# A weighted sum over eight experts: four terms of each tail token on TensorE, paired tail loads, two tail stores, and six tokens of one round stored from GpSimd

## The chip, the cores and the metric

The kernel runs on one core of a Trainium2 chip. The metric is the device time of one execution in microseconds (us); the median of five runs is compared. Where one execution was profiled, its own time and its span (first to last instruction on the core's engines) are given beside it, and all durations below are from that execution.

The engines of the core that matter here: VectorE (DVE in the profile), TensorE (PE, with its weight loads as PEld), ScalarE (ACT), GpSimd (POOL) and SyncE (SP). SP, ACT and POOL each issue DMA transfers, on a queue of their own (q1, q10 and q0 in the profile), and one set of 16 DMA engines carries all of them.

## The reference

```python
def setup_inputs():
    batch, seq, n_experts, expert_dim = 16, 1024, 8, 512
    ...
def reference(expert_outputs, combine_weights):
    weights = combine_weights[..., np.newaxis]
    return np.sum(expert_outputs * weights, axis=2).astype(np.float32)
```

Each of 16 x 1024 = 16384 tokens has eight rows of 512 float32 numbers and eight weights; the output is the weighted sum of the eight rows. 268 MB are read and 33.5 MB written, and there is no reuse.

## The kernel before

Every one of the 128 partitions owns 128 tokens (`T_P`). 120 of them (`LOOP`) are done in 12 rounds (`ROUNDS`) of ten tokens (`R`), the other eight (`TAIL`) after that, in the *tail*.

**Buffers.** `ring` holds the ten tokens of one round, eight rows each (16 KB for a token and partition). It is a single buffer: as soon as VectorE has finished the tokens of a chunk, SP loads the next round's chunk into their place. The chunks of a round have 4, 4 and 2 tokens (`CHUNKS`). `acc` holds the results of two rounds, ten tokens (of 2 KB each) in each half. `w_t` holds all weights, `w_c` a copy of the weights of two rounds that ScalarE makes for each round (L167).

**A round** (loop at L219, VectorE alone): for each chunk one `tensor_tensor` (L225) multiplies row 0 of all its tokens by their weights, and then seven `scalar_tensor_tensor` for each token (L215, `fused`) multiply a row by its weight and add it to `acc`. The tokens of a pair are taken in turn, so that an instruction doesn't wait for the one just before it. The last term of a token counts up the semaphore `done`, by which everything else knows how many tokens are finished.

**Loads** are issued by SP in the order of the program (`loads_and_last_stores`): each waits for the `done` count of the tokens whose place it takes. After the 36 chunks of the rounds come eight loads of the tail, one for each token `j` (L142); each waits for the token of the last-but-one place in `ring`, `LOOP - R + j + 1`. Then SP issues the store of the last round (L97) and the stores of the tail (L146), each after its wait on `done`. SP is one instruction stream, so all of this keeps its order, and its transfers are worked off in their order by each DMA engine.

**Stores** of rounds 0 to 9 are one transfer each, issued by ScalarE (L97), which then waits for an earlier one to land before it overwrites the weights' copy. The store of round 10 (`ROUNDS - 2`) is cut up: ScalarE issues four tokens and two tokens over all partitions (L173), and the last four as pairs for 8 partitions (L174); GpSimd issues those pairs for the other 120 partitions (`OURS`, L116). GpSimd also issues two tiny loads into `spare` (`turn`, L121, of 4 and 13 partitions), whose data nobody reads. A transfer over 120 partitions is spread over 15 of the 16 DMA engines.

**The tail.** Eight tokens, each a sum of eight terms. The first `pe_e[j]` of them (6, 6, 6, 6, 5, 5, 5, 4) are made by TensorE: ScalarE writes a diagonal matrix with the weight on its diagonal (`diag`, four buffers, L179), and a matmul with the token's row as moving data (L191) adds weight times row into `ps` in PSUM. [...] ScalarE starts on the diagonals only when all parts of round 10's store have landed (`last_out`, `pairs_out`), since VectorE's tail results go into the same places of `acc`. VectorE adds the remaining terms: `fused` with `ps` as the first addend (waiting for `product`, which counts matmuls), then with `acc`. For tokens 2 to 6 every one of these waits for the one before it. For token 7 VectorE starts from `ring` (L259) and adds `ps` at the very end (L266). Tail stores are of 4, 2, 1 and 1 tokens (`tail_stores`).

What decides the place of the PE terms is this list:

```python
    pe_e = [6, 6, 6, 6, 5, 5, 5, 4]
    tail_stores = [(0, 4), (4, 2), (6, 1), (7, 1)]
    diags = [(j, e) for j in range(TAIL) for e in range(pe_e[j])]
```

## Time and profile before

| | |
|---|---|
| median of 5 runs | 707.05 us (706.75 to 707.31) |
| profiled execution: its time / its span | 707.32 us / 705.1 us |
| VectorE busy | 642.9 us, 91% of the span, 898 instructions |
| TensorE busy, all of it in the tail | 39.9 us, 86 passes (43 matmuls) |
| ScalarE busy | 21.2 us, of it 16.9 us for 43 diagonals |
| GpSimd busy | 2.7 us |
| moved by DMA | 302.54 MB, mean 429 GB/s |
| share of 16 DMA engines' time: SP's queue / ACT's / POOL's | 90.0% / 9.2% / 0.3% |

The span is cut into slices in the profile, and the mean busy share of the 16 DMA engines is 9 tenths or more in all of the 40 slices but the last, where it is 8. VectorE is at 9 tenths or so up to the last two slices, where it is at 5; TensorE works only in the last three. So there are two parts: 672 us of rounds in which the DMA engines are full and VectorE nearly so, and a tail of 33 us in which TensorE, VectorE and the DMA engines all have their share. The change touches what happens from 619.7 us on, where round 10 is finished.

### The profile page before, as it was taken

What the parts mean: (1) busy time and instruction counts of PE and PEld (TensorE: products, weight loads), DVE (VectorE), ACT (ScalarE), POOL (GpSimd) and SP (SyncE); (2) the same over time, 40 slices, a digit from 0 to 9 for tenths busy, and PEclk for the clock granted to TensorE, in tenths of its full rate; (3) what the DMA queues carried; (4) which work ended last, traced back from release to release, by engine and by line L of the source; (5) the groups of instructions that cost most, each with busy time, mean ns of one, the idle gap of its engine ahead of it and who ended that gap; (6) DMA issues with size and microseconds to landing.
All of it is one profiled execution on the core that took longest, in us unless ns stands there. A gap on an engine that the chain in (4) does not pass through costs nothing. (4 is left out here: it accounts for less than half of the span.)

```text
span 705.1 us, 1333 instructions
## 1 busy us (share of the span) xinstructions
PE 39.9 (6%) x86; PEld 17.3 (2%) x86; DVE 642.9 (91%) x898; ACT 21.2 (3%) x56; POOL 2.7 (0%) x9
## 2 busy tenths in 40 slices
PE   0000000000000000000000000000000000000696
PEld 0000000000000000000000000000000000000242
DVE  0599999989999989989989998998998998999955
ACT  0000000000000000000000000000000000000242
POOL 0000000000000000000000000000000000000000
PEclk9999999999999999999999999999999999999998
DMA  9999999999999999999999999999999999999998
GB/s 413 390 472 417 398 437 444 416 448 426 435 434 459 423 412 448 435 425 464 434 393 463 420 424 438 465 402 465 420 445 418 420 431 431 468 407 413 435 429 347
DMA packets 9690, 302.54 MB, mean 429 GB/s; under 512 B 1240, under 2 KB 1624, under 8 KB 2392
## 3 DMA queue, kind: packets, MB, share of 16 engines
q1 hardware_dynamic: 7600, 273.68, 90.0%
q10 hardware_dynamic: 1752, 27.85, 9.2%
q0 software_dynamic: 336, 0.98, 0.3%
q14 instruction: 2, 0.02, 0.0%
HBM read 268.96 MB, written 33.55 MB: 429 GB/s over the span
## 5 line engine op out<-in xcount | busy, mean ns | idle before, releaser
L215 DVE SCALAR_TENSOR_TENSOR acc<-ring,w_c,acc 128x512 f32<-128x512 f32 x840 | 559.7, 747 | 1.3
L225 DVE TENSOR_TENSOR acc<-ring,w_c 128x2048 f32<-128x2048 f32 (+1 forms) x36 | 69.6, 1933 | 43.6 <-DVEq L201 43.6
L191 PE MATMUL ps<-ring,diag 128*128 128x512 f32 x86 | 39.9, 628 | 658.5 <-DMA ring<-in_expert_outputs_dram 658.5
L191 PEld LDWEIGHTS ps<-ring,diag 128*128 128x128 f32 x86 | 17.3, 203 | 680.2 <-DMA ring<-in_expert_outputs_dram 658.5
L167 ACT COPY w_c<-w_t 128x80 f32<-128x80 f32 x12 | 3.0, 258 | 587.1 <-DMA out_dram<-acc 564.8
L179 ACT ACTIVATE diag<-ident,w_t 128x128 f32<-128x128 f32 x43 | 16.9, 400 | 86.2 <-DMA out_dram<-acc 64.4
L215 DVE SCALAR_TENSOR_TENSOR acc<-ring,w_t,ps 128x512 f32<-128x512 f32 x7 | 5.1, 747 | 12.6 <-PE ps L191 12.6
L215 DVE SCALAR_TENSOR_TENSOR acc<-ring,w_t,acc 128x512 f32<-128x512 f32 x13 | 9.7, 751 | 0.4
L116 POOL DMA_DIRECT2D out_dram<-acc x1 | 0.8, 754 | 617.5 <-DVE acc L215 617.5
L167 ACT ACT_TABLE_LOAD x1 | 1.3, 1283 | 0.9 <-SPq L270 0.9
L121 POOL DMA_DIRECT2D spare<-in_combine_weights_dram x2 | 1.3, 645 | 0.3 <-issue 0.3
L266 DVE TENSOR_TENSOR acc<-acc,ps 128x512 f32<-128x512 f32 x1 | 0.7, 689 | 0.1
L259 DVE TENSOR_SCALAR acc<-ring,w_t 128x512 f32<-128x512 f32 x1 | 0.5, 482 | 0.0
L150 POOL TENSOR_SCALAR_AFFINE_SELECT ident<-ident 128x128 f32<-128x128 f32 x1 | 0.3, 287 | 0.1
L149 POOL MEMSET ident<- 128x128 f32 x1 | 0.2, 204 | 0.5 <-SPq L270 0.5
L291 POOL MEMSET const-bfloat16-1.0<- 128x1 bf16 x1 | 0.1, 96 | 0.0
L291 POOL MEMSET const-uint8-127<- 128x1 uint8 x1 | 0.1, 96 | 0.0
L291 POOL MEMSET const-float32-0.0<- 128x1 f32 x1 | 0.1, 93 | 0.2 <-issue 0.2
L291 POOL MEMSET const-float32-1.0<- 128x1 f32 x1 | 0.1, 93 | 0.0
## 6 DMA issues: line engine op xcount, KB each, us to landing
ring<-in_expert_outputs_dram SPq DMA_DIRECT2D x12, 4096.0 KB, 34.0
out_dram<-acc ACTq DMA_DIRECT2D x10, 2560.0 KB, 26.7
ring<-in_expert_outputs_dram SPq DMA_DIRECT2D x8, 2048.0 KB, 29.5
out_dram<-acc SPq DMA_DIRECT2D x1, 2560.0 KB, 26.8
out_dram<-acc ACTq DMA_DIRECT2D x1, 1024.0 KB
out_dram<-acc SPq DMA_DIRECT2D x1, 1024.0 KB, 17.3
out_dram<-acc POOLq DMA_DIRECT2D x1, 960.0 KB, 33.6
out_dram<-acc ACTq DMA_DIRECT2D x1, 512.0 KB
```

What stands on the lines that cost most here:

```text
L116: gpsimd.dma_start(out=o_r[0:OURS], in_=a_r[0:OURS]).then_inc(pairs_out, 16)
L121: gpsimd.dma_start(out=spare[0:k, b : b + 4].rearrange("p (i j) -> p i j", i=2)[:, :, 0:1], in_=w[0 : 2 * k].rearrange("(p i) e -> p i e", ...
L149: gpsimd.memset(ident, 0.0).then_inc(id_set, 1)
L150: gpsimd.affine_select(out=ident, in_=ident, compare_op=mybir.AluOpType.not_equal, fill=1.0, base=0, pattern=[[-1, P]], channel_multiplier ...
L167: scalar.copy(out=w_c[:, h * R : h * R + R], in_=w_t[:, n * R : n * R + R]).then_inc(w_set[h], 1)
L179: i = scalar.mul(out=diag[:, k % DIAGS], in_=ident, mul=w_t[:, LOOP + j, e : e + 1])
L191: tensor.matmul(ps[:, j], lhsT=diag[:, k % DIAGS], rhs=ring[:, j, e], start=e == 0, stop=e == pe_e[j] - 1,).then_inc(product, 1)
L215: return vector.scalar_tensor_tensor(out=acc[:, g], in0=ring[:, g % R, e], scalar=weight, in1=before, op0=mult, op1=add)
L225: i = vector.tensor_tensor(out=acc[:, q : q + m], in0=ring[:, r : r + m, 0], in1=w_c[:, q : q + m, 0:1].to_broadcast([P, m, D]), op=mult,)
L259: i = vector.tensor_scalar_mul(out=acc[:, j], in0=ring[:, j, e], scalar1=weight)
L266: i = vector.tensor_tensor(out=acc[:, j], in0=acc[:, j], in1=ps[:, j], op=add)
L291: nc = _bacc.Bacc("TRN2", target_bir_lowering=False, num_devices=1)
```

## The change

Four things are changed, and all of them lie behind round 10.

1. TensorE makes the first four terms of each tail token (`K = 4`) in place of 6, 6, 6, 6, 5, 5, 5, 4. That is 32 matmuls and 32 diagonals in place of 43, and 33 VectorE instructions in the tail in place of 22.
2. The first six tail tokens are loaded as three pairs. A pair waits for the `done` count of its second token. There are five loads and five semaphores in place of eight.
3. The tail is stored as two transfers of four tokens.
4. Round 10's ten tokens are taken as two halves of five. ScalarE stores the first two of each half, over all partitions, in one transfer. GpSimd stores the last three of each half (six tokens, rows of 6 KB): first for 120 partitions, then, after a tiny load of 5 partitions, for the other 8. ScalarE waits for its own transfer and for GpSimd's four (two tiny loads, two stores) before it starts on the diagonals.

```diff
+    SPLIT = 2
...
-    pe_e = [6, 6, 6, 6, 5, 5, 5, 4]
-    tail_stores = [(0, 4), (4, 2), (6, 1), (7, 1)]
-    diags = [(j, e) for j in range(TAIL) for e in range(pe_e[j])]
+    K = 4
+    tail_loads = [(0, 2), (2, 2), (4, 2), (6, 1), (7, 1)]
+    tail_stores = [(0, 4), (4, 4)]
+    diags = [(j, e) for j in range(TAIL) for e in range(K)]
...
-    tail_in = [sem(f"tail_in{j}") for j in range(TAIL)]
+    tail_in = [sem(f"tail_in{k}") for k in range(len(tail_loads))]
...
+    def halves(n, first, last):
         s = n % 2 * R
-        for r, m in ((0, 4), (6, 2)):
-            yield o_g[n // 4, n // 2 % 2, :, s + r : s + r + m], acc[:, s + r : s + r + m]
-        pairs = [
-            a[:, s + 2 : s + 10].rearrange("p (b k) d -> p b (k d)", k=4)[:, :, 2 * D :]
+        return [
+            a[:, s : s + R].rearrange("p (b k) d -> p b (k d)", b=2)[:, :, first * D : last * D]
             for a in (o_g[n // 4, n // 2 % 2], acc)
         ]
...
+    def store_halves(gpsimd):
+        o_r, a_r = halves(ROUNDS - 2, SPLIT, R // 2)
         turn(gpsimd, 4, 0)
         gpsimd.wait_ge(done, (ROUNDS - 1) * R)
-        o_r, a_r = list(parts(ROUNDS - 2))[2]
-        gpsimd.dma_start(out=o_r[0:OURS], in_=a_r[0:OURS]).then_inc(pairs_out, 16)
-        turn(gpsimd, 13, 4)
+        gpsimd.dma_start(out=o_r[0:OURS], in_=a_r[0:OURS]).then_inc(rest_out, 16)
+        turn(gpsimd, 5, 4)
+        gpsimd.dma_start(out=o_r[OURS:P], in_=a_r[OURS:P]).then_inc(rest_out, 16)
...
-        for j in range(TAIL):
-            sync.wait_ge(done, LOOP - R + j + 1)
-            sync.dma_start(out=ring[:, j], in_=x_t[:, j]).then_inc(tail_in[j], 16)
+        for k, (j, m) in enumerate(tail_loads):
+            sync.wait_ge(done, LOOP - R + j + m)
+            sync.dma_start(out=ring[:, j : j + m], in_=x_t[:, j : j + m]).then_inc(tail_in[k], 16)
...
-        *both, (o_r, a_r) = parts(ROUNDS - 2)
-        for o_p, a_p in both:
-            scalar.dma_start(out=o_p, in_=a_p).then_inc(last_out, 16)
-        scalar.dma_start(out=o_r[OURS:P], in_=a_r[OURS:P]).then_inc(last_out, 16)
-        scalar.wait_ge(last_out, 48)
-        scalar.wait_ge(pairs_out, 48)
+        o_r, a_r = halves(ROUNDS - 2, 0, SPLIT)
+        scalar.dma_start(out=o_r, in_=a_r).then_inc(last_out, 16)
+        scalar.wait_ge(last_out, 16)
+        scalar.wait_ge(rest_out, 64)
...
-            if e == 0:
-                tensor.wait_ge(tail_in[j], 16)
+            if (j, e) in starts:
+                tensor.wait_ge(tail_in[starts[j, e]], 16)
...
-                    if e == pe_e[j]:
+                    if e == K:
                         i = fused(j, e, weight, ps[:, j])
-                        i.wait_op(product, sum(pe_e[: j + 1]), "sem-ge")
+                        i.wait_op(product, K * (j + 1), "sem-ge")
```

The remaining lines of the diff follow from these: `range(K, E)` for `range(pe_e[j], E)`, `stop=e == K - 1`, `starts` (the load that a token's first matmul waits for), `tail_in[-1]` for token 7's first VectorE instruction, and `rest_out` for `pairs_out`.

## The prediction

> **What bounds the kernel now.** I read first the busy time by stretches of the tail, whose columns are the stretch, its length, busy time (and count) of PE, PEld, DVE, ACT and POOL, the granted TensorE clock, the DMA share and GB/s.

> ```profile
> 690.00:692.00 2.00, 2.00 (x6) 0.95 (x5) 1.31 (x2) 1.00 (x3) 0.00 (x0) 1.00 1.08 461
> 698.00:700.00 2.00, 0.34 (x1) 0.00 (x0) 1.93 (x3) 0.00 (x0) 0.00 (x0) 1.00 0.98 412
> ...
> 700.00:701.00 1.00, 0.00 (x0) 0.00 (x0) 0.72 (x2) 0.00 (x0) 0.00 (x0) 1.00 0.99 397
> 701.00:702.00 1.00, 0.00 (x0) 0.00 (x0) 0.00 (x0) 0.00 (x0) 0.00 (x0) 0.74 0.71 272
> 702.00:703.00 1.00, 0.00 (x0) 0.00 (x0) 0.00 (x0) 0.00 (x0) 0.00 (x0) 0.50 0.47 178
> 703.00:704.00 1.00, 0.00 (x0) 0.00 (x0) 0.00 (x0) 0.00 (x0) 0.00 (x0) 0.50 0.02 8
> ```

> The DMA engines are full until 701 and run empty by 703.4. So even a tail without compute could not end much earlier. The chain of waits (start, us, what) tells which compute ends last:

> ```profile
> 630.65 27.76 DMA ring<-in_expert_outputs_dram
> 658.41 0.04 issue
> 658.46 36.46 PE ps L191 x78
> 694.92 0.02 issue
> 694.95 0.76 DVE acc L215
> ...
> 700.14 0.69 DVE acc L266
> ```

> From the landing of token 0 (658.41) to 694.92 TensorE works without a gap; the rest is VectorE. VectorE's timeline shows the same from the other side, as idle time in brackets:

> ```profile
> 673.21 1.41 DVE L215 SCALAR_TENSOR_TENSOR acc<-ring,w_t,acc 128x512 f32<-128x512 f32 x2
> 676.92 0.75 DVE L215 SCALAR_TENSOR_TENSOR acc<-ring,w_t,ps 128x512 f32<-128x512 f32 x1 [2.30 <-PE ps L191]
> ...
> 694.95 0.75 DVE L215 SCALAR_TENSOR_TENSOR acc<-ring,w_t,ps 128x512 f32<-128x512 f32 x1 [1.97 <-PE ps L191]
> 695.73 1.54 DVE L215 SCALAR_TENSOR_TENSOR acc<-ring,w_t,acc 128x512 f32<-128x512 f32 x2
> 697.18 0.48 DVE L259 TENSOR_SCALAR acc<-ring,w_t 128x512 f32<-128x512 f32 x1
> 697.70 2.33 DVE L215 SCALAR_TENSOR_TENSOR acc<-ring,w_t,acc 128x512 f32<-128x512 f32 x3
> 700.14 0.69 DVE L266 TENSOR_TENSOR acc<-acc,ps 128x512 f32<-128x512 f32 x1
> ```

> The last add ends at 700.83, SP issues the last store at 700.85, it lands 3.0 us later (its row in the out_dram view) at 703.84, and 1.29 us of closing work make 705.13. The packets inside those 3.0 us, one per partition: the first start 0.83 us after the issue, an engine has eight of 2 KB at 0.08 us, so most engines are through at 702.4. One DMA engine, still at the earlier tail stores until 702.74, ends at 703.39; 0.45 us later its part has landed. So the compute chain and one late DMA engine end within 1 us of each other.

> **The change, part by part.**

> *Fewer terms on TensorE.* A matmul is two passes, 0.429 us apart at full clock: 11 fewer are 11 x 0.858 = 9.4 us off TensorE. VectorE gets 11 x 0.747 (row of L215) = 8.2 us more. If VectorE never waited from 672.0 (end of its rounds) on: tokens 0 and 1 in turn, 8 x 0.705; tokens 2 to 6, 20 dependent ones at 0.775 (three took 694.95 to 697.27); token 7 as now, 3.56 from the end of token 6 (697.27 to 700.83). Sum 24.7, end at 696.7. That is the floor of this edit, 4.1 us below today's 700.83, if the data were there.

> *Paired loads.* It isn't. A pair is issued with its second token, 0.66 us later than its first now (630.65 and 631.32), which is hidden by the queue in front of it: these loads land 26.5 to 32.5 us after their issue. But the first token of a pair now lands with the second. Issue plus time to landing of tokens 1, 3, 5, 6, 7 today: 631.32 + 32.0 = 663.3, 640.59 + 32.5 = 673.1, 652.20 + 30.7 = 682.9, 660.81 + 27.0 = 687.8, 661.47 + 31.2 = 692.7. Bytes are the same; a 16 KB packet takes 0.611 us and a 32 KB one 1.213, so an engine saves 48 x 0.611 - 24 x 1.213 = 0.2 us.

> *Round 10's store.* For fifteen engines nothing changes in sum: 8 packets of 8 KB (0.309), 8 + 16 of 4 KB (0.159) make 6.3 us; then 16 of 4 KB and 16 of 6 KB (0.234, between the 4 and 8 KB rows) again 6.3. The engine left out has 1.2 us less, but it lands first already (0.7 us ahead of the middle), and a transfer waits for its last engine. The 8 odd partitions put two packets on each of eight engines, 0.47 us now against 0.32; the trace doesn't name the engines, so a late one may gain 0.32 or lose 0.47. With the 0.2 saved, the pair (4, 5) lands between 682.3 and 683.1; I take 682.7, as the late engine is likelier in both groups or in neither than newly in. ScalarE issues two transfers fewer (0.36 to 0.59 us each) and GpSimd one more (0.56 to 0.75); behind them on either engine stand only the waits of the next part, which end 36 us later.

> *The new wait.* ScalarE's diagonals wait for GpSimd's second store too; behind them wait TensorE and VectorE. Today the last part lands at 656.58 and the diagonals start at 656.60. GpSimd's last five queue entries (end marks, tiny load, two rows) now take turns with tail packets of 1.213 instead of 0.611: + 5 x 0.6, plus the larger rows, so about 659.9. Four diagonals (1.28) later it is 661.2, before the pair lands at 663.1: hidden, with 2 us to spare; without that cover it would delay TensorE one for one.

> *The chain.* TensorE starts at 663.2, at half clock for 5.5 us as now (passes 0.853 apart from 658.46 to 663.7). Pair 1's 16 passes: 6.4 slow, 9.6 at 0.429, end 672.8; pair 2 has just landed (672.9) and ends at 679.8; then TensorE stands still for 2.9 us, which it never does now. Token 4's product: 682.7 + 0.05 + 7 x 0.429 + 0.593 (last pass) + 0.04 = 686.4. VectorE is free by then (tokens 0 and 1 until 678.4 since token 1's product comes at 673.4, tokens 2 and 3 until 684.6). Products of tokens 5, 6, 7 follow 3.43 apart: 689.8, 693.3, 696.7, their loads being there. VectorE: token 6 from 693.3, 3.1 us, 696.4; token 7 + 3.56: 699.95. Of the 4.1 us, 0.9 is left: the rest goes into waiting for loads.

> *Two tail stores.* The first four tokens are issued at about 684.6 and wait in the queue anyway. The last store has 1 MB instead of 256 KB: 8 packets of 0.309 = 2.48 against 0.64, so 1.84 us on the path. In return 512 and 256 KB (8 x 0.159 + 8 x 0.08 = 1.9 us) are gone from the queue in front of the late engine, which becomes free at about 700.7 and no longer counts. Sum: 699.95 + 0.02 + 0.83 + 2.48 = 703.28, landing 0.2 to 0.45 later, 1.29 of closing: 704.9. Against the span of 705.13 that is -0.2 us. The profiled execution took 707.32, 0.27 above the median; I take the difference off the median: 706.85.

> *The clock.* The granted clock is the unknown. The stretch 701 to 702 shows 0.74, so full clock ended at 701.5, 3.15 us after the last pass (698.34). A pause of 2.9 us lies just under that, and no shorter one is in the trace. Bounds: nothing (no pause inside the burst now costs any clock), or all of the restart, 5.5 us at half clock = 2.75 us. I take nothing, as the only loss seen came after more.
> [...]

> **The rivals.**

> *The clock drops in the pause* (slower). Place: between pairs 2 and 3. For it: 2.9 against 3.15 us, and the drop's moment needn't be fixed to the burst. Against: the pause is the shorter. Tokens 4 to 7 are chained to it, so all of 2.75 reaches the end: 709.6; with half of it 708.2. It decides from 1.6 us of loss on. 22%.

> *The diagonals come late* (slower). If GpSimd's last rows land after 665, TensorE's first pair ends after 675, and from 1.8 us more (VectorE's slack before token 4, 684.6 against 686.4) the end moves: 3 us late at the end would be 709.9. Against: 3 us of margin in all. 4%.

> *VectorE is the bound and the loads aren't* (faster). Floor 696.7 and the same 4.95 behind it: span 701.65, time 703.6. Against: the DMA share of 0.98 to 1.08 leaves the loads no room to land 4 us earlier. Halfway, with the late engines gone (the middle ones have token 5 at 681.7, 1.2 earlier than the last), it is 705.8, still near my bound. 10% for beyond it.

> *It does as costed*, gains and losses cancelling: 62%, own range 706.0 to 707.7; another 2% I can't name, slower.

> **How the numbers follow.** About 0.2% (1.4 us) is what a measurement of this kernel can tell from no change. Slower than that: 22 + 4 + 2 = 28%; faster 10%; within 62%. The time is the likeliest case's, 706.85. The range goes down to 706.0 (lower bound of the landing, 0.4 earlier, and quicker landing of the last store) and up to 708.7, into the lesser clock losses; some 8% are left out below and 12% above.

> **What would show it.** In the profile after: VectorE through 672 without change; pair landings at 663, 673 and 683; TensorE idle about 2.9 us before pair 3 and full clock behind it; VectorE waiting for TensorE at tokens 4, 5 and 6 and ending near 700; the last store landing 3.5 us or so after its issue; DMA share falling before 700 and rising once more. Wrong: passes 0.85 apart after 683, the first pass well after the first landing, VectorE ending below 698.5, or a last store much longer than 3.6 us.

## The result and the profile after

The changed kernel takes 708.18 us (median of 26 runs) against 706.94 for the kernel before (46 runs): a ratio of 1.0012, 95% interval 1.0006 to 1.0017. That is slower by 0.12%, less than the 0.2% that the prediction took as the bound, but beyond the interval, and the forecast was 706.85, a little faster.

The median hides the main thing. The 26 runs fall into two groups with nothing between them: eight from 706.41 to 706.90 (median 706.5) and eighteen from 708.10 to 708.65 (median 708.2), 1.7 us apart. The kernel before has no such groups (706.63 to 707.34). The profiled execution, 708.37 us with a span of 706.6, is one of the upper group.

The busy time by stretches shows what happened there. The granted clock changes at 682.02 and at 685.44, and 678.61 lies as far ahead of the first change as that from the second; the columns are those of the prediction. Below, a *stretch* is a window of that length, 3.41 us.

```profile
678.61:682.02 3.41, 1.16 (x3) 0.19 (x1) 3.27 (x6) 0.80 (x2) 0.00 (x0) 1.00 0.93 399
682.02:685.44 3.42, 3.09 (x4) 1.50 (x5) 1.50 (x2) 0.40 (x1) 0.00 (x0) 0.50 0.98 414
685.44:690.00 4.56, 4.56 (x12) 1.92 (x11) 2.29 (x4) 2.01 (x5) 0.00 (x0) 1.00 1.03 439
698.00:700.00 2.00, 0.00 (x0) 0.00 (x0) 1.91 (x3) 0.00 (x0) 0.00 (x0) 1.00 0.64 270
700.00:701.00 1.00, 0.00 (x0) 0.00 (x0) 0.89 (x2) 0.00 (x0) 0.00 (x0) 1.00 0.00 0
...
702.00:703.00 1.00, 0.00 (x0) 0.00 (x0) 0.00 (x0) 0.00 (x0) 0.00 (x0) 0.75 1.11 467
703.00:704.00 1.00, 0.00 (x0) 0.00 (x0) 0.00 (x0) 0.00 (x0) 0.00 (x0) 0.50 1.03 418
```

From 682.02 to 685.44 the granted clock is 0.50, with full clock before and after. The pair (4, 5) lands at 682.31, just inside, and its first passes are 0.85 us apart, where they are 0.43 apart behind 685.69. The other new thing is the DMA share: 0.64, then nothing at all from 700 to 701, then full again from 702. The DMA engines, which had work until 701 in the kernel before, now stand still until the packets of the last store start, at 701.99.

The timeline (start, length, engine and line, idle time before in brackets) has the pause and what it does to VectorE:

```profile
662.93 16.84 PE L191 MATMUL ps<-ring,diag 128*128 128x512 f32 x32 [662.93 <-DMA ring<-in_expert_outputs_dram]
...
682.35 15.51 PE L191 MATMUL ps<-ring,diag 128*128 128x512 f32 x32 [2.58 <-DMA ring<-in_expert_outputs_dram]
...
687.60 0.75 DVE L215 SCALAR_TENSOR_TENSOR acc<-ring,w_t,ps 128x512 f32<-128x512 f32 x1 [4.05 <-PE ps L191]
...
700.45 0.69 DVE L266 TENSOR_TENSOR acc<-acc,ps 128x512 f32<-128x512 f32 x1
```

TensorE pauses once, for 2.58 us, before the pair (4, 5). Token 4's product reaches VectorE at 687.60. At full clock it takes 3.74 us from the first pass (682.37 to 686.11 in experiment 4's profile), which would be 686.1; here it took 5.25. The products of tokens 5 and 6 follow 3.44 and 3.43 us apart (691.04 and 694.47), as costed, and VectorE ends at 701.14.

The chain of waits has the same story in order; its line for TensorE has shrunk from 36.46 us to 12.10, and ahead of it stands a load instead of TensorE's own work:

```profile
652.35 29.96 DMA ring<-in_expert_outputs_dram
682.31 0.04 issue
682.35 12.10 PE ps L191 x24
694.45 0.02 issue
694.47 0.76 DVE acc L215
...
700.45 0.69 DVE acc L266
```

### The profile page after: what moved, and what is told of

The parts are those of the page before. It is cut to its first block, busy times and chain, and to the rows that moved or that the text cites. A ratio compares the mean times of both kernels' runs of the same rounds, so it can differ in the third digit from the quotient of the medians.

```text
span 706.6 us, 1280 instructions
## 1 busy us (share of the span) xinstructions
PE 32.4 (5%) x64; PEld 13.6 (2%) x64; DVE 650.7 (92%) x909; ACT 16.8 (2%) x45; POOL 3.3 (0%) x10
## 5 line engine op out<-in xcount | busy, mean ns | idle before, releaser
L215 DVE SCALAR_TENSOR_TENSOR acc<-ring,w_c,acc 128x512 f32<-128x512 f32 x840 | 559.8, 747 | 1.3
L191 PE MATMUL ps<-ring,diag 128*128 128x512 f32 x64 | 32.4, 669 | 665.5 <-DMA ring<-in_expert_outputs_dram 665.5
L191 PEld LDWEIGHTS ps<-ring,diag 128*128 128x128 f32 x64 | 13.6, 217 | 683.5 <-DMA ring<-in_expert_outputs_dram 667.1
L215 DVE SCALAR_TENSOR_TENSOR acc<-ring,w_t,acc 128x512 f32<-128x512 f32 x24 | 17.6, 750 | 0.6
L178 ACT ACTIVATE diag<-ident,w_t 128x128 f32<-128x128 f32 x32 | 12.5, 400 | 90.0 <-DMA out_dram<-acc 68.9
L215 DVE SCALAR_TENSOR_TENSOR acc<-ring,w_t,ps 128x512 f32<-128x512 f32 x7 | 5.2, 745 | 4.7 <-PE ps L191 4.7
L266 DVE TENSOR_TENSOR acc<-acc,ps 128x512 f32<-128x512 f32 x1 | 0.7, 689 | 0.1
L259 DVE TENSOR_SCALAR acc<-ring,w_t 128x512 f32<-128x512 f32 x1 | 0.5, 482 | 0.0
```

What stands on the lines that cost most here:

```text
L178: i = scalar.mul(out=diag[:, k % DIAGS], in_=ident, mul=w_t[:, LOOP + j, e : e + 1])
L191: tensor.matmul(ps[:, j], lhsT=diag[:, k % DIAGS], rhs=ring[:, j, e], start=e == 0, stop=e == K - 1,).then_inc(product, 1)
L215: return vector.scalar_tensor_tensor(out=acc[:, g], in0=ring[:, g % R, e], scalar=weight, in1=before, op0=mult, op1=add)
L259: i = vector.tensor_scalar_mul(out=acc[:, j], in0=ring[:, j, e], scalar1=weight)
L266: i = vector.tensor_tensor(out=acc[:, j], in0=acc[:, j], in1=ps[:, j], op=add)
```

## The experiments

All but the sixth and seventh were timed against the kernel before on the same chip in five rounds, those two in three. "Changed" below is the changed kernel, "five terms" the one of experiment 2. Experiments 1 to 4, 5 to 8 and 9 to 11 ran on three chips, on which the kernel before had medians of 706.90, 706.94 and 706.86 us, so 0.1 or 0.2 us between experiments of different chips say little. Only 6, 7 and 11 have an interval that leaves out 1; what the others show is in how their runs spread and in their profiles.

| | kernel | median us (lowest to highest, runs) | ratio to before, 95% interval | VectorE ends / last landing / span, profiled |
|---|---|---|---|---|
| | before | 706.94 (706.63 to 707.34, 46) | 1 | 700.83 / 703.84 / 705.1 |
| | changed | 708.18 (706.41 to 708.65, 26) | 1.0012 (1.0006 to 1.0017) | 701.14 / 705.03 / 706.6 |
| 1 | changed, two filler matmuls | 706.64 (706.41 to 707.05, 11) | 0.9995 (0.9986 to 1.0004) | 699.83 / 703.71 / 705.3 |
| 2 | five terms for tokens 2 and 3 | 706.68 (706.53 to 706.85, 11) | 0.9997 (0.9988 to 1.0006) | 699.53 / 703.42 / 705.0 |
| 3 | changed, single tail loads | 706.38 (706.18 to 706.68, 11) | 0.9993 (0.9984 to 1.0002) | 697.41 / 702.82 / 704.4 |
| 4 | changed, old store of round 10 | 707.06 (706.51 to 708.91, 11) | 1.0008 (0.9999 to 1.0017) | 699.65 / 703.52 / 705.1 |
| 5 | five terms, four tail stores | 706.47 (706.25 to 706.74, 11) | 0.9994 (0.9985 to 1.0003) | 699.49 / 703.03 / 704.6 |
| 6 | changed, old TensorE terms | 711.68 (711.09 to 712.76, 4) | 1.0073 (1.0057 to 1.0088) | 703.73 / 707.61 / 708.9 |
| 7 | three terms for tokens 2 and 3 | 708.15 (707.83 to 709.49, 9) | 1.0019 (1.0009 to 1.0029) | 701.94 / 705.82 / 707.2 |
| 8 | before, four terms alone | 706.73 (706.59 to 706.84, 11) | 0.9997 (0.9988 to 1.0006) | 697.72 / 703.22 / 704.8 |
| 9 | single loads, old store of round 10 | 706.75 (706.68 to 706.98, 11) | 0.9998 (0.9989 to 1.0007) | 697.80 / 703.33 / 704.9 |
| 10 | single loads, four tail stores | 706.63 (706.51 to 706.98, 11) | 0.9996 (0.9987 to 1.0005) | 698.11 / 703.62 / 705.2 |
| 11 | the kernel of 4 again | 708.51 (706.81 to 708.73, 11) | 1.0019 (1.0010 to 1.0028) | 699.59 / 703.46 / 705.0 |

### 1. Filler in the pause

```diff
         for k, (j, e) in enumerate(diags):
+            if (j, e) == (4, 0):
+                for f in range(2):
+                    tensor.matmul(ps[:, TAIL - 1], lhsT=ident, rhs=ring[:, 3, f], start=True, stop=True)
             if (j, e) in starts:
```

> The changed kernel, with two matmuls more on TensorE between the pairs (2, 3) and (4, 5), into the PSUM place of token 7 that its own first matmul starts afresh. Theory (clock): the change's loss is the half clock granted from 682.0 to 685.4 us, caused by TensorE's pause of 2.6 us. Four passes more (1.7 us) leave a pause of about 0.9 us: the granted clock stays at 1.0 through the tail, VectorE ends at about 699.4 in place of 701.14, span about 704.8, time about 706.5 in every run (none near 708.2). Rival (last store): the loss is the last store of 1 MB, 3.9 us from issue to landing against 3.0, so nothing changes: about 708.2. Rival (landing): it is the later landing of paired loads: 708.2 too.

The upper group is gone: eleven runs, none above 707.05. The stretch that ends 13.65 us behind the rise to full clock (669.04 in this trace), where the clock fell in the changed kernel's profile (668.37 to 682.02), shows the two matmuls as TensorE's time, and the clock stays at 1.00:

```profile
679.28:682.69 3.41, 2.63 (x7) 0.90 (x6) 3.27 (x6) 0.76 (x2) 0.00 (x0) 1.00 0.90 384
```

Pair (4, 5) landed at 682.51 here, so nearly all of those 2.63 us are ahead of it; without the four passes (4 x 0.429 us) about 0.9 would be left, by estimate. Work that nobody needs makes the kernel 1.5 us faster, so the loss is TensorE's clock, and neither the last store nor the landing of the pairs, which are unchanged.

### 2. Useful work in the pause

```diff
-    K = 4
+    pe_e = [4, 4, 5, 5, 4, 4, 4, 4]
```

with `pe_e[j]` for `K` at its uses.

> The changed kernel, with five terms on TensorE in place of four for tokens 2 and 3: real work in the pause. Theory (clock): pair (2, 3) takes 20 passes, 8.6 us, the pause shrinks to about 0.9 us, the clock stays at 1.0; VectorE ends at about 699.4, time about 706.5 in every run. Rivals (last store, landing): about 708.2, since nothing behind token 4 is changed.

As expected by the theory: the pause is 0.86 us, the clock holds (0.996 over the profiled span, against 0.995 in the changed kernel's profile), and all eleven runs are within 0.3 us of each other. It is the same gain without wasted work.

### 3. Single tail loads

```diff
-    tail_loads = [(0, 2), (2, 2), (4, 2), (6, 1), (7, 1)]
+    tail_loads = [(j, 1) for j in range(TAIL)]
```

> The changed kernel with the eight tail loads of one token that the kernel before has. Theory (clock): a token of four terms takes 3.4 us of TensorE and loads land 4.9 us apart, so the pauses are 1.4 us each and the clock stays at 1.0; token 5's product no longer waits behind token 4's, VectorE ends at about 697.9; the last store then starts earlier, up to where the late DMA engine is free: span about 704.0 to 704.6, time 705.9 to 706.4. Rival (last store): the path ends with the same 1 MB, so about 1 us is gained from VectorE's earlier end at most and 707 to 708 is seen. Rival (half clock whenever TensorE pauses at all): clock 0.5 through much of the tail, VectorE ends after 701, 708 or more.

The best time seen: the highest of its eleven runs (706.68) lies just below the lowest of 33 of the kernel before on the same chip (706.70), though the interval of the ratio reaches 1.0002. TensorE has five pauses of 1.18 to 1.20 us and keeps full clock, so it isn't any pause that costs the clock; each has 3.70 us of passes behind it, so any stretch of 3.41 us has at least 2.21 us of TensorE's time in it (two of them, 668.95 to 672.36 and 675.77 to 679.18, show 2.22 and 2.21 at a clock of 1.00). VectorE ends at 697.41, 3.4 us earlier than in the kernel before, but the last landing moves by 1.0 us only (703.84 to 702.82). The busy time by stretches says why:

```profile
698.00:700.00 2.00, 0.00 (x0) 0.00 (x0) 0.00 (x0) 0.00 (x0) 0.00 (x0) 0.92 1.00 422
700.00:701.00 1.00, 0.00 (x0) 0.00 (x0) 0.00 (x0) 0.00 (x0) 0.00 (x0) 0.50 1.04 442
701.00:702.00 1.00, 0.00 (x0) 0.00 (x0) 0.00 (x0) 0.00 (x0) 0.00 (x0) 0.50 0.76 320
```

No engine computes any more, and the DMA engines are full until past 701: here they are the bound, and VectorE's time is free.

### 4 and 11. Round 10's old store

`halves` and `store_halves` are replaced by `parts` and `store_pairs` of the kernel before, and ScalarE's waits with them; the rest of the change stays.

> The changed kernel with round 10's store as in the kernel before (ScalarE four and two tokens, GpSimd the four others for 120 partitions). Theory (clock): this part costs nothing either way; time 708.2 (or 706.5 in runs whose clock happens to hold), as for the changed kernel. Rival (new wait): GpSimd's second store and its landing at 661.2 are what delays TensorE: the first pass comes earlier than 662.9 and the time falls by a part of 1.2 us. Rival (balance): the engine left out of six tokens instead of four lets the loads land earlier; without it, pair (4, 5) lands 0.3 to 0.5 us later than 682.3 and the time is higher by that.

> Round 10's old store in the changed kernel, a second time on this chip. Theory (phase of the clock's stretches, not the store): again two groups of runs 1.7 us apart, around 706.8 and 708.5, in whatever proportion. Rival (the old store holds the clock): mostly the lower group again, as in 7 of 11 runs before.

Two groups again, near 706.9 and 708.5: seven and four runs at first, three and eight the second time. The medians of one and the same kernel, 707.06 and 708.51, differ by more than the whole change, as they only say which group had the majority. The granted clock that each run lists, a mean over its span, goes with the groups: 0.993 to 0.995 in all 30 runs of the upper groups of this and the changed kernel, 0.996 to 0.998 in 14 of the 18 of the lower ones (0.995 in the other four). This part of the change neither makes nor cures the loss. The diagonals do start earlier with the old store (659.28 against 661.28), but the pair lands after both, at 662.90 and 662.89. And both profiled executions here kept their clock, with the same pause (2.58 and 2.59 us, against 2.58 in the changed kernel). The first two rows are experiment 4's, the third is experiment 11's:

```profile
677.18:680.59 3.41, 2.61 (x7) 0.83 (x5) 3.30 (x5) 1.61 (x4) 0.00 (x0) 1.00 1.03 447
680.59:684.00 3.41, 1.63 (x4) 0.87 (x5) 2.30 (x4) 0.40 (x1) 0.00 (x0) 1.00 0.96 408
...
680.42:683.83 3.41, 1.51 (x4) 0.80 (x5) 2.53 (x4) 0.35 (x1) 0.00 (x0) 1.00 0.93 399
```

The first row ends 13.65 us behind the rise to full clock in its trace (666.94), the distance at which the clock fell in the changed kernel's profile (668.37 to 682.02). The second is the stretch behind it, and so is the third (the rise of experiment 11 is at 666.77). In experiment 4 the pause (679.8 to 682.4) is cut in two by that moment, 0.80 us ahead of it and 1.78 behind it, and the emptier of the two stretches still has 1.63 us (1.51 in experiment 11) of TensorE's time. In the changed kernel's profile 2.25 us of the pause lay ahead of the fall (679.77 to 682.02), in a stretch that had 1.16. (A stretch laid around the whole pause would have 0.83 in each of them.) So with one and the same pause the clock is lost in some executions and kept in others, and what the profiles differ in is where the pause lies, counted from the rise. The rise isn't at a fixed distance from TensorE's first pass: it comes 5.4 us behind it in the changed kernel's profile (662.93 to 668.37) and 4.0 in experiment 4's (662.9 to 666.94). That the place of the pause makes the two groups is my estimate from these three profiles; what sets the moment of a change isn't shown.

### 5. Four tail stores again

On top of experiment 2: `tail_stores = [(0, 4), (4, 2), (6, 1), (7, 1)]`.

> The kernel with five terms for tokens 2 and 3 (clock held, 706.68), and the four tail stores of the kernel before (4, 2, 1, 1 tokens). Theory (the last store costs a part of the gain): only 256 KB are left behind VectorE's end at about 699.5; a last store of 1 MB took 3.9 us from issue to landing there, one of 256 KB 3.0 in the kernel before; the rest of the data goes out while VectorE works. The last landing comes at about 702.5 in place of 703.42, span about 704.1, time 705.8 to 706.0. Rival (the DMA engines are full anyway): the last landing can't come before about 702.8, as with single loads, so 0.4 us at most are gained: 706.3.

The last landing moves from 703.42 to 703.03 and the median by 0.2 us, which the two intervals don't tell from nothing. That is the rival's size. The last store is issued at the same time (699.5), but the stores ahead of it keep the DMA engines full: their share from 699 to 701 is 0.96 and 0.98 in the two microseconds, against 0.47 and 0.62 in experiment 2.

### 6. The old TensorE terms with paired loads

The `pe_e` list of the kernel before in the changed kernel.

> The changed kernel with the terms on TensorE of the kernel before (6, 6, 6, 6, 5, 5, 5, 4). Theory: with paired loads TensorE starts 4.5 us later than in the kernel before (662.9 against 658.46) and works 36.5 + 3.4 us without a pause, so its clock holds and all of the delay reaches the end: VectorE ends at about 705.2, and the last store of 1 MB adds its 3.9 us: span about 710.7, time 712.4. Rival (TensorE isn't what limits the tail; the DMA engines are): the time stays within 1 us of 707.

Slower by 0.73%, as the theory has it in kind; VectorE ends at 703.73 in the profile (the fastest of the four runs), 1.5 us before my figure, since TensorE started 0.3 us sooner than costed and was at full clock 3.0 us later (665.59) and not 5.5. Pairing needs fewer terms on TensorE: without them, 2.9 of the 4.2 us by which TensorE starts later reach VectorE's end, and the time grows by 4.7 us.

### 7. A longer pause

```diff
-    K = 4
+    pe_e = [4, 4, 3, 3, 4, 4, 4, 4]
```

> The changed kernel with three terms on TensorE for tokens 2 and 3, which lengthens the pause before pair (4, 5) from 2.6 to about 4.4 us. Theory (a stretch of 3.41 us with little work on TensorE takes the clock away, and where the stretches begin differs from run to run): now nearly every run has such a stretch, so the two values of the changed kernel (708.2 and 706.5) become one: all runs at 708.0 to 709.3. Rival (the two values come from something else, the pause only coincides): two values as before, with 706.5 in a third of the runs.

All nine runs lose: none is below 707.83. Five are at 707.8 to 708.2, and four at 708.5 to 709.5, where the granted clock averages less over the span (0.991 against 0.993 to 0.995). The profile, one of the latter, shows two stretches at half clock:

```profile
677.06:680.47 3.41, 0.74 (x2) 0.00 (x0) 3.27 (x6) 0.73 (x2) 0.00 (x0) 1.00 1.06 456
680.47:683.89 3.42, 1.78 (x2) 0.84 (x3) 3.31 (x5) 0.00 (x0) 0.00 (x0) 0.50 0.89 378
683.89:687.30 3.41, 3.41 (x5) 1.35 (x4) 0.81 (x2) 0.80 (x2) 0.00 (x0) 0.50 1.01 425
```

Behind the stretch with 0.74 us of TensorE's time the clock is at half; behind the next, with 1.78, it is still at half, through a third in which TensorE is busy for all of the 3.41 us. The pause is 4.3 us here, against 2.58 in the changed kernel, and the lower group is gone.

### 8, 9 and 10. The parts apart

8: `pe_e = [4, 4, 4, 4, 4, 4, 4, 4]` in the kernel before, nothing else. 9: experiment 3 with round 10's old store. 10: experiment 3 with the four tail stores.

> The kernel before with four terms for each tail token and nothing else of the change. Theory (the fewer terms are what gains, the DMA engines then set the end): pauses of 1.4 us, clock held, VectorE ends near 697.7, the last landing at 702.8 to 703.4 instead of 703.84, since one DMA engine is late in this kernel; span 704.2 to 704.7, time 705.9 to 706.4. Rival (the paired loads, two stores and the new store of round 10 bring the gain over the kernel before): 706.9 as before.

> Single tail loads (706.38) with round 10's store as in the kernel before. Here the DMA engines are full to the end, so that their latest one decides. Theory (leaving one engine out of six tokens evens the engines out): without it the latest engine is 0.7 us or so behind the middle, as in the other two kernels with the old store, in place of 0.25; time 706.7. Rival (that part of the change does nothing): 706.4.

> Single tail loads (706.38) with the four tail stores of the kernel before. Theory (the DMA engines end last, all data is in the queue by 697.5): no difference, 706.3 to 706.5. Rival (the last store's size is on the path): 0.5 to 1 us less, below 705.9.

Fewer terms alone: VectorE ends 3.1 us earlier, the median falls by 0.2 us (the interval reaches 1.0006), less than expected (706.73 against 706.4 at most). In the profile two DMA engines are still late: half of the engines have landed their part of the last store by 702.45, the last two at 703.14 and 703.22. Experiment 9 has one such engine (702.46 and 703.33). With six tokens left out of one engine, the latest is only 0.27 us behind the middle (experiment 3: 702.55 and 702.82), and the median is 0.4 us lower. That would speak for the new store of round 10, but it isn't shown: the intervals of 3, 8 and 9 overlap, 3 ran on another chip than 9, and experiment 10, with that store, had its latest engine 0.69 behind. In 10 the four tail stores brought nothing, as expected where the DMA engines end last.

## Why the prediction was wrong

**The step that failed** is the one on the clock: "I take nothing, as the only loss seen came after more." The kernel before lost its clock 3.15 us after TensorE's last pass, and I read that as a length a pause must reach. The runs don't bear that out: the changed kernel lost its clock 2.25 us after a pass, in a pause of 2.58, and experiments 4 and 11 kept it through 2.58 and 2.59 in the executions that were profiled. What the profiles show beside the length is how little TensorE did in the 3.41 us ahead of a loss: 0.27 us in the kernel before (698.07 to 701.49), 1.16 in the changed one and 0.74 in experiment 7, where the stretches quoted for experiments 1, 4 and 11, whose profiles kept it, have 1.51 at the least, laid by the rise of the clock. The named rival, at 22%, was right, and in the right place: the clock drops in the pause, between pairs 2 and 3; 18 of 26 runs lie in the group of the profile that shows it, and a sign that the prediction named for being wrong, passes 0.85 us apart after 683, is in that profile.

**Its size was off too.** I priced the loss at 2.75 us, the whole slow start, or half of that. The 3.41 us at half clock cost 1.5 us in the profile (5.25 against 3.74 us to token 4's product), about half of the 3.09 us that TensorE worked in them, and the gap between the two groups is 708.2 - 706.5 = 1.7.

**Right, in the runs that kept their clock:** 706.5 there, against 706.85. No run of the changed kernel's lower group was profiled; in the profiles of experiments 4 and 11, which differ from it in round 10's store, VectorE ended at 699.6 (I had 699.95). In the changed kernel's own profile the pairs landed at 662.89, 672.59 and 682.31 (663.1, 672.9, 682.7), the pause was 2.6 (2.9), and VectorE waited for tokens 4, 5 and 6 (4.05, 0.32 and 0.32 us). Of the 4.1 us from 700.83 down to the floor of 696.7, 1.2 were gained in experiments 4 and 11; the rest went into waiting for loads, as costed, and with single loads VectorE ended at 697.41.

**Right, with a size off:** the diagonals began at 661.28, not at about 659.9 (what that sum missed isn't shown), and the four were there at 662.56, 0.3 us before the first pair and not 2. The cover held, barely. The last store took 3.9 us from issue to landing (3.5 to 3.75 by my sum).

**Right as a reason, shown by 3 and 8:** the DMA engines bound the end when VectorE doesn't. Taking 3 us off VectorE's end brought the last landing 0.6 to 1.0 us forward, and the medians are 0.2 to 0.5 us lower.

**Missed:** the closing work. It grew from 1.29 to 1.56 us.

## What to carry to other kernels

Where TensorE works in bursts, don't take the length that stood ahead of one drop of the clock in a trace as what a pause must reach: here that was 3.15 us, and the changed kernel, with 2.58 in its profile, has 18 of 26 runs in the upper group. Look at every run rather than the median, which hid the two groups here. Give TensorE real work in the pause (experiment 2 left 0.86 us of it, and its highest run was 706.85), or split the pause into smaller ones: eight loads of one token, with pauses of 1.2 us, kept the clock where three pairs lost it. Before taking work off the last engine of a tail, look whether the DMA engines are full to the end there; if so, an earlier end of that engine brings little (3 us brought 1.0 us at most here).

## What the runs showed of the hardware

```profile
694.69:698.10 3.41, 1.22 (x3) 0.19 (x1) 2.85 (x4) 0.00 (x0) 0.00 (x0) 1.00 0.96 410
698.10:701.52 3.42, 0.00 (x0) 0.00 (x0) 0.00 (x0) 0.00 (x0) 0.00 (x0) 0.50 0.98 400
```

Of the 48 runs of the changed kernel and of experiments 4 and 11, whose profiles have a pause of 2.58 or 2.59 us, 30 are in the upper groups, 62.5%.
- TensorE's time in a stretch at half clock, and what came behind it: with 3.09 us (the changed kernel, 682.02 to 685.44) full clock came, with 1.78 (experiment 7, 680.47 to 683.89) it didn't. At the start of the burst the stretch with 2.07 us in the kernel before (657.12 to 660.53) and that with 2.02 in the changed one (661.54 to 664.95) left the clock at half; behind the next one, all of it TensorE's time, it was full (663.94 and 668.37). Ahead of the first recorded change the clock's column shows 1.00; the half clock is read there from the passes, which are 0.85 us apart.
- The closing takes 1.26 to 1.34 us after the last landing in three kernels (before, experiments 6 and 7) and 1.56 to 1.60 in all others. The first three have two transfers of the instruction queue within the span, the others a third, of 8 KB, in the closing: the page's line is the first below for experiment 6, the second for experiment 8.

```profile
q14 instruction: 2, 0.02, 0.0%
```

```profile
q14 instruction: 3, 0.02, 0.0%
```

In the closing of the changed kernel ScalarE's first two drains start 0.39 us apart (705.25 and 705.64), in that of the kernel before 0.09. The third transfer starts only at 706.31, behind that gap, so the two come together, and what makes the gap stays open. A shorter program of ScalarE isn't the whole of it: experiment 7 has the fewest diagonals (30) and is among the short closings.
- Two sets of eleven runs of one kernel gave medians 1.45 us apart (experiments 4 and 11), and neither's interval holds the other's ratio: an interval made for runs that scatter evenly says little where a kernel's runs fall into two groups.
